# One of seven Strassen products of the up/gate stage computed by a second, inner Strassen scheme

## The chip, the cores and the metric

One NeuronCore of one Trainium2 chip runs the whole kernel. The metric is the time of one execution on the device, in microseconds (us). The kernel before took 1171.3 us, the median of three runs (1171.29 to 1173.07).

## The reference, cut to what matters

The reference is one residual block of a streaming encoder on 1024 tokens of width 1024: a normalisation, a mixer (gated DeltaNet heads and a short convolution), a second normalisation and a SwiGLU feed-forward of width 2816, then a last normalisation. The change lies in the first half of the feed-forward:

```python
def swiglu(h, w_gate, w_up, w_down):
    return (jax.nn.silu(h @ w_gate) * (h @ w_up)) @ w_down
...
h = rms_norm(x, norm2_w[l]) * (1.0 + scale2) + shift2
x = x + gate2 * swiglu(h, w_gate[l], w_up[l], w_down[l])
```

## The kernel before

**Numbers.** A float32 operand of a large matmul is split into a high part (a cast to the rounded matmul type, on ScalarE, called ACT) and a low part (the rest, a subtraction on VectorE, called DVE). A product is then three matmuls: high by high, high by low, low by high. Each has a weight load of its own.

**The up/gate stage.** The 2816 columns of w_gate and w_up are 22 tiles of 128, handled as 11 pairs p = 0 to 10. For a pair, the weights are cut into two column tiles by two inner halves (A11 to A22, 4 inner blocks k of 128 each), and the normalised tokens into two inner halves by two token halves of 512 (B11 to B22). A Strassen scheme makes the four blocks of the result with seven products instead of eight. `STEPS` (L44) lists them: step 0 is A11 x B11 into bank X, step 1 is A12 x B21 into bank Y, step 2 S2 x T2 onto X, step 3 S1 x T1 into Z, step 4 S3 x T3 onto X, step 5 S4 x B22 onto Z, step 6 A22 x T4 onto X. S1 to S4 are sums of weight blocks, T1 to T4 of token blocks. Each step is done for gate (q = 0) and up (q = 1), each into a PSUM bank of its own: `run` (L1719) issues 2 q x 4 k x 3 = 24 matmuls with 512 columns.

B11 and B21 lie in `H[0..3][0]` and `H[4..7][0]`: they are made by `first_half` (L1551), in the stage before, by transposing the normalised tokens on TensorE (PE), adding the shift and splitting (`tr_split`, L1527). The T blocks come from `sums_x` (L1541) and from `t_split` (L1700), which runs during pair 0 only, between the products of pair 0, into PSUM banks that are named by hand.

**Order of work.** From the second normalisation on there is no planner: each engine works in the order in which the program is written. Around the change that order is: the output products of the mixer (`w_out_tile`), tile by tile, with `first_half`, `early_load`, `sums_x` and the normalisation of the tiles between them; then pair 0, written out step by step with `t_split` (from L1908 on); then the loop over p = 1 to 10 (L1956), in which each step calls `run(p, s)` and then `block(p, s)` (L1790). `block` holds what DVE and ACT do while that step's products run: sums, casts (`cast`, L1672) and lows (`low`, L1678) of the weights for a later step, and the reading of the banks. `keep` (L1739) copies a bank to SBUF (ACT), `close` (L1744) adds a bank to the copy (DVE). In block 1, `keep(p, "p1", "X")` copies X after step 0; in block 2, `close(p, "p1", "Y")` adds Y after step 1, and then SiLU of the gate (ACT) and the product with up (DVE) follow. The casts and lows of A12 for pair p + 1 stand in block 6 of pair p. In block 0 of the next pair the last two banks X are read, the first by ACT, the second by DVE. Stores to DRAM and weight loads go by the SyncE queue (SP); `early_load` (L1576) uses ACT's queue. `slot` (L1689) hands out split weight tiles in a ring of eight.

Of the kernel before, what the change touches and what calls it, by code (L numbers as in the profile page):

```python
# [17 lines left out]
P = 128  # L18
# [5 lines left out]
HT = 512  # L24
# [27 lines left out]
def kernel(  # L52
# [21 lines left out]
    nc = tc.nc  # L74
    chain, mover = [None], [None]

    class Ordered:
# [18 lines left out]
    PE, DVE, ACT, POOL, SP = (Ordered(n, e) for n, e in (  # L96
        ("pe", nc.tensor), ("dve", nc.vector), ("act", nc.scalar), ("pool", nc.gpsimd), ("sp", nc.sync)))
# [7 lines left out]
    def nm(s):  # L105
        n_id[0] += 1
        return f"{s}_{n_id[0]}"
# [5 lines left out]
    cst = ctx.enter_context(tc.tile_pool(name="cst", bufs=1))  # L113
    hp_ = ctx.enter_context(tc.tile_pool(name="hp", bufs=1))
# [16 lines left out]
    def flat(ap):  # L131
        return ap.rearrange("p a b -> p (a b)")
# [37 lines left out]
    def raw_t(shape=(P, HT), dtype=F32):  # L170
        return cyclic("raw", RAW, shape, dtype)
# [372 lines left out]
    s2c = cst.tile([P, KB], F32, name="s2c", tag="s2c")  # L544
    b2c = cst.tile([P, KB], F32, name="b2c", tag="b2c")
    db2 = cst.tile([P, 4], F32, name="db2", tag="db2")
    su = []

    sim = Sim(seq, dict(pe=T_START[0], dve=T_START[1], act=T_START[2], pool=T_START[3], sp=T_START[4]))
# [794 lines left out]
    Y = [{}, {}]  # L1344
# [206 lines left out]
    def first_half(ks):  # L1551
        for k in ks:
            H[k][0] = tr_split(lambda: h_slot(k, 0), [x2n[i][:, k * P:(k + 1) * P] for i in range(4)], allb.get("tr"), b2c[:, k:k + 1])

    def w_out_tile(t, ch):
        ps = allb.get("o")
        sl = slice((t - 4) * P, (t - 3) * P)
        us = (us0, us1)[ch]
        for n, k in enumerate(KORD):
            for m, (yi, ui) in enumerate(((0, 0), (0, 1), (1, 0))):  # L1560
                pmm(ps, Y[1][k][yi][:, sl], us[k][ui], n == 0 and m == 0, n == KB - 1 and m == 2)
        cs = slice(ch * HT, (ch + 1) * HT)
        DVE.tensor_tensor(x2[t][:, cs], x2[t][:, cs], ps, ALU.add)
# [32 lines left out]
    first_half(range(4))  # L1596
    w_out_tile(5, 1)
    keep_x2(5, (1,))
    first_half(range(4, 8))
    early_load(0)  # L1600
    early_load(1)
    sums_x(0)
# [25 lines left out]
    class Weights:  # L1628
# [53 lines left out]
        def mat(self, n):  # L1682
            for q in range(2):
                self.cast(n, q)
                self.low(n, q)

    n_slot = [0]

    def slot():  # L1689
        n_slot[0] += 1  # L1690
        n = n_slot[0] - 14
        if n <= 0 or n % 8 in (5, 6, 7, 0):
            return hl_t([P, 2, 4, P])
        return mp.tile([P, 2, 4, P], F32R, name=nm("u"), tag="gl", bufs=4)
# [24 lines left out]
    def run(p, s, q_=(0, 1)):  # L1719
        b, an, bn, first = STEPS[s]  # L1720
        if first and 0 in q_:
            for q in (0, 1):
                bk[p][q][b] = bank_tile(bk[p][q][b], "acc")
        for q in q_:
            u, ps = W[p].u[an][q], bk[p][q][b]
            for k in range(4):
                x_ = B[bn][k]
                for n, (wi, xi) in enumerate(((0, 0), (0, 1), (1, 0))):
                    pmm(ps, u[:, wi, k, :], x_[:, xi, :], first and k == 0 and n == 0, k == 3 and n == 2, not first)

    def cc(p, n):
        if p == 0 and n == "p1":
# [6 lines left out]
    def keep(p, n, b):  # L1739
        cc(p, n)  # L1740
        for q in (0, 1):
            ACT.copy(c[p][n][q], bk[p][q][b])

    def close(p, n, b):  # L1744
        for q in (0, 1):
            DVE.tensor_tensor(c[p][n][q], c[p][n][q], bk[p][q][b], ALU.add)

    def silu(p, n):
        ACT.activation(c[p][n][0], c[p][n][0], AF.Silu)
# [10 lines left out]
    def store(p, n, t):  # L1760
        pend.append((am_scr[p, A_IX[n]], t))
# [28 lines left out]
    def block(p, s):  # L1790
        w, n = W.get(p), W.get(p + 1)
        last = p == NP - 1
        if s == 0:
            if p > 0:
                o = p - 1
                ACT.activation(c[o]["z5"][1], bk[o][0]["X"], AF.Silu)
            if w:
                w.sum_n("S1")
                w.sum_n("S2")
                for q in (0, 1):  # L1800
                    w.cast("S2", q)
            if p > 0:
                a12 = c[o]["z5"][1]
                DVE.tensor_tensor(a12, bk[o][1]["X"], a12, ALU.mult)
                store(o, "A12", a12)
            if w:
                for q in (0, 1):
                    w.low("S2", q)
        elif s == 1:
            if w:  # L1810
                keep(p, "p1", "X")
                w.cast("S1", 0)
                w.cast("S1", 1)
            if p > 0:
                o = p - 1
                a11, s1, a21 = c[o]["p1"][0], c[o]["p1"][1], c[o]["u2"][0]
                DVE.tensor_tensor(a11, s1, a11, ALU.subtract)
                DVE.tensor_tensor(a21, c[o]["z5"][1], a11, ALU.subtract)
                store(o, "S2", a11)
                store(o, "S4", a21)  # L1820
            if w:
                w.low("S1", 0)
                w.low("S1", 1)
                w.sum_n("S3")
        elif s == 2:
            close(p, "p1", "Y")
            w.cast("S3", 0)
            silu(p, "p1")
            w.cast("S3", 1)
            w.low("S3", 0)  # L1830
            w.low("S3", 1)
            act(p, "p1")
            store(p, "A11", c[p]["p1"][0])
            w.sum_n("S4")
        elif s == 3:
            keep(p, "u2", "X")
            w.mat("S4")
            prep_gate(p - 1)
        elif s == 4:
            keep(p, "z5", "Z")  # L1840
            w.mat("A22")
            prep_sums(p - 1)
            if last:
                first_mats(0, "A11", am_scr)
        elif s == 5:
            close(p, "z5", "X")
            if n:
                n.cast("A11", 0)
            silu(p, "z5")
            if n:  # L1850
                n.cast("A11", 1)
                n.low("A11", 0)
                n.low("A11", 1)
            act(p, "z5")
            store(p, "A22", c[p]["z5"][0])
            if last:
                first_mats(1, "B11", None)
        elif s == 6:
            close(p, "u2", "Z")
            if n:  # L1860
                n.cast("A12", 0)
            silu(p, "u2")
            if n:
                n.cast("A12", 1)
                n.low("A12", 0)
                n.low("A12", 1)
            act(p, "u2")
            a11, a21, a22, s1, s3 = c[p]["p1"][0], c[p]["u2"][0], c[p]["z5"][0], c[p]["p1"][1], c[p]["u2"][1]
            DVE.tensor_tensor(s1, a21, a22, ALU.add)
            DVE.tensor_tensor(s3, a11, a21, ALU.subtract)  # L1870
            store(p, "S1", s1)
            store(p, "S3", s3)
            if last:
                first_mats(2, "A12", am_scr)

# [48 lines left out]
    W[0].low("S2", 1)  # L1924
    t_split("T1", (6, 7, 4, 5))
    close(0, "p1", "Y")
    silu(0, "p1")
    run(0, 2, (0,))
    act(0, "p1")
# [26 lines left out]
    for p in range(1, NP):  # L1956
        for s in range(7):
            if s == 0:
                prep_load(p - 1)
            if s == 3 and p < NP - 1:  # L1960
                W[p + 1] = Weights(p + 1)
                W[p + 1].load(0)
            if s == 5 and p < NP - 1:
                W[p + 1].load(1)
            if p == NP - 1 and s in (3, 5, 6):
                first_load(*{3: (0, "A11"), 5: (1, "B11"), 6: (2, "A12")}[s])
            if s != 6:
                flush()
            run(p, s)
            block(p, s)  # L1970
    m_ctx.__exit__(None, None, None)
    dp = ctx.enter_context(tc.tile_pool(name="dp", bufs=1, side="left", reuse_waits="tile"))
# [211 lines left out]
```

## Time and profile before

| | |
|---|---|
| median of three runs | 1171.3 us |
| the profiled execution's own time | 1170.96 us |
| its span in the profile | 1169.1 us |
| instructions | 16455 |
| granted TensorE clock, mean | 0.999 |
| DVE, additions of PSUM banks (close) | 43.9 us in 66 |
| ACT, copies of banks (keep) | 38.4 us in 66 |

The profile is one execution. PE is TensorE's matmuls, PEld its weight loads, which overlap them; SP is the queue that issues DMAs. A row of the timeline gives the start in us from the span's start, the length, the engine, the line, the operation with output and inputs, and, in brackets, how long the engine had been idle and what ended the wait. Rows of one kind in a row are merged (x24); the ends of matmuls are modelled, so spacing is best read from starts. A row by groups gives busy us, mean ns of one, and idle time before.

### The profile page before, as it was taken

The numbers are of one execution on the slowest core, as the hardware profiler recorded it, in microseconds if no ns is written. First come the engines' busy times: TensorE is split into PE (matmuls) and PEld (weight loads), VectorE is DVE, ScalarE is ACT, GpSimd is POOL, SyncE is SP. The second block draws the span as 40 slices with busy tenths as digits, with TensorE's granted clock in tenths as the row PEclk, the third lists the DMA queues.
The fourth block names the chain that finished last, engine by engine and source line by source line (L and its number), as shares of the span: only waits on it lengthen the run. The fifth ranks groups of instructions, "written<-read, shape, count | busy, mean of one in ns | idle before, by whom it ended". The sixth has DMA issues, their size and how long they took to land.

```text
span 1169.1 us, 16455 instructions
## 1 busy us (share of the span) xinstructions
PE 1159.0 (99%) x5586; PEld 969.4 (83%) x5586; DVE 922.0 (79%) x1718; ACT 539.5 (46%) x1168; POOL 61.2 (5%) x100
## 2 busy tenths in 40 slices
PE   9999999999999999999999999999999999999997
PEld 7888888888888988888888888888888888888886
DVE  7998988899977998668776777776777687788676
ACT  5688733469633643325433333333333365443343
POOL 2110101002000002100000000000000000000002
PEclk9999999999999999999999999999999999999999
DMA  9624365535215554434264456446554589869413
GB/s 360 257 64 146 106 186 158 174 116 161 81 57 163 164 187 153 194 97 139 95 214 151 149 199 225 151 139 221 192 182 135 197 303 391 310 203 339 146 36 144
DMA packets 126452, 207.06 MB, mean 177 GB/s; under 512 B 20512, under 2 KB 45088, under 8 KB 126368
## 3 DMA queue, kind: packets, MB, share of 16 engines
q1 hardware_dynamic: 120992, 202.80, 51.3%
q10 hardware_dynamic: 5376, 3.21, 0.9%
q8 instruction: 44, 0.72, 0.3%
q14 instruction: 40, 0.33, 0.1%
HBM read 150.91 MB, written 55.05 MB: 176 GB/s over the span
## 4 chain that ended last, share of the span: by engine, by line
PE 92%; DVE 4%; DMA 2%; ACT 1%; issue 1%; SPq 0%; POOL 0%; DVEq 0%; ACTq 0%; POOLq 0%
PE acc L88 34%; PE acc L450 24%; PE dn L88 17%; PE o L450 4%; PE o L88 4%; PE A L450 1%; PE K L450 1%; DVE xo L89 1%; PE ab L450 1%; PE tr L450 1%; PE w L450 1%; PE u L450 1%; PE qk L450 1%; PE kk L450 1%; DMA R<-in_w_gate_dram 1%
## 5 line engine op out<-in xcount | busy, mean ns | idle before, releaser
L450 PE MATMUL acc<-h,u 128*128 128x512 f32 x1200 | 300.2, 398 | 0.0
L450 PEld LDWEIGHTS acc<-h,u 128*128 128x128 f32 x1200 | 219.2, 188 | 41.6
L88 PE MATMUL acc<-h,hl 128*128 128x512 f32 x600 | 140.1, 390 | 0.0
L88 PEld LDWEIGHTS acc<-h,hl 128*128 128x128 f32 x600 | 112.4, 188 | 23.2
L88 PE MATMUL acc<-h,u 128*128 128x512 f32 x456 | 106.1, 389 | 0.0
L88 PE MATMUL acc<-T,hl 128*128 128x512 f32 x432 | 101.4, 390 | 0.1
L88 PEld LDWEIGHTS acc<-h,u 128*128 128x128 f32 x456 | 85.6, 188 | 17.8
L88 PEld LDWEIGHTS acc<-T,hl 128*128 128x128 f32 x432 | 80.9, 188 | 17.2 <-ACT cc L89 0.5
L88 PE MATMUL dn<-h,h 128*128 128x512 f32 x396 | 90.7, 389 | 0.0
L89 DVE TENSOR_TENSOR xo<-xo,dn 128x512 f32<-128x512 f32 x84 | 57.2, 686 | 42.0 <-PE dn L88 34.6
L89 ACT COPY cc<-acc 128x512 f32<-128x512 f32 x66 | 38.4, 590 | 108.3 <-PE acc L88 108.3
L88 PEld LDWEIGHTS dn<-h,h 128*128 128x128 f32 x396 | 74.3, 188 | 15.4
L88 PE MATMUL acc<-T,u 128*128 128x512 f32 x360 | 84.0, 389 | 0.0
L88 PEld LDWEIGHTS acc<-T,u 128*128 128x128 f32 x360 | 67.6, 188 | 14.0
L89 DVE TENSOR_TENSOR cc<-cc,acc 128x512 f32<-128x512 f32 x66 | 43.9, 684 | 29.8 <-PE acc L88 29.8
L450 DVE TENSOR_TENSOR u<-raw,u 128x512 fp32r<-128x512 f32 x82 | 56.3, 688 | 12.2 <-ACT u L450 12.0
L89 DVE TENSOR_TENSOR hl<-R,hl 128x512 fp32r<-128x512 f32 x60 | 39.5, 689 | 33.5 <-ACT hl L89 33.4
L450 ACT CAST u<-raw 128x512 fp32r<-128x512 f32 x61 | 37.8, 621 | 57.8 <-PE acc L450 52.9
L450 DVE SCALAR_TENSOR_TENSOR cv<-pr,cols_a,cv 128x512 f32<-128x512 f32 x72 | 53.2, 747 | 0.3 <-ACT cv L450 0.2
L89 ACT CAST h<-rw 128x512 fp32r<-128x512 f32 x57 | 32.7, 618 | 40.9 <-PE dn L88 34.6
L89 DVE TENSOR_TENSOR u<-R,u 128x512 fp32r<-128x512 f32 x46 | 30.1, 688 | 20.5 <-ACT u L89 20.5
L89 ACT CAST hl<-R 128x512 fp32r<-128x512 f32 x60 | 35.5, 622 | 23.1 <-DVE R L89 10.7
(339 smaller groups left out, 2002.0 us busy)
## 6 DMA issues: line engine op xcount, KB each, us to landing
raw<-in_w_in_dram SPq DMA_DIRECT2D x82, 256.0 KB, 3.1
am_scr<-cc SPq DMA_DIRECT2D x77, 256.0 KB, 4.5
raw<-in_w_ada_dram SPq DMA_DIRECT2D x56, 256.0 KB, 3.2
rw<-am_scr SPq DMA_DIRECT2D x55, 256.0 KB, 5.1
rw<-bm_scr SPq DMA_DIRECT2D x53, 256.0 KB, 5.3
bm_scr<-raw SPq DMA_DIRECT2D x51, 256.0 KB, 5.4
R<-in_w_gate_dram SPq DMA_DIRECT2D x22, 512.0 KB, 3.9
R<-in_w_up_dram SPq DMA_DIRECT2D x22, 512.0 KB, 5.3
```

Source lines behind the costliest of these rows:

```text
L88: return call(*a, **k)
L89: ins = call(*a, **k)
L450: ins = call(*a, **k)
```

## The change

For p = 1 to 10, step 1 (A12 x B21 for gate and up) is done by seven smaller products m1 to m7 with 256 columns. The inner scheme cuts three ways: its rows are gate and up, its inner halves are k = 0, 1 and k = 2, 3, its columns the two token halves of 256. Pair 0 keeps its step 1. The 24 matmuls of 512 columns become 7 x 2 x 3 = 42 of 256; m1, m2, m5, m6 and m3 are issued in step 1, m7 after the q = 0 half of step 2, and m4 after its q = 1 half. They use the two banks of Y: one holds y and z (256 columns each), the other x. Four times a part is copied out by ACT between products that go onto it (K).

New operands: `inner_half` replaces `first_half(range(4, 8))` and makes, besides H[4..7][0], three sums q1, q2, q3 of token blocks of 256 with their splits; `inner_last`, in pair 0 after `close(0, "p1", "Y")`, makes q4 in the place of the second token half of H[4] and H[5]. For each pair `inner_sums` makes four sums of weight blocks (DVE) in block 6, and four casts and lows of them replace the two of A12 (three of 512 columns, one of 256). `close_inner` replaces `close` in block 2; as m4 is issued at the end of step 2, its last addition needs the end of step 2. `keep(p, "p1", "X")` moves ahead of the products of step 1. The SBUF area reserved for dynamic DMAs is made smaller.

```diff
@@ the stage before
+    HN = HT // 2
+    tq = {n: hp_.tile([P, 2, 2, HN], F32R, name=n, tag=n) for n in ("q1", "q2", "q3")}
+
+    def inner_half(a):
+        DVE.tensor_tensor(db3[:, a:a + 1], b2c[:, 6 + a:7 + a], b2c[:, 4 + a:5 + a], ALU.subtract)
+        bank = {}
+        for k in (4 + a, 6 + a):
+            bank[k] = allb.get("tr")
+            H[k][0] = tr_split(lambda: h_slot(k, 0), [x2n[i][:, k * P:(k + 1) * P] for i in range(4)], bank[k], b2c[:, k:k + 1])
+        pa, pb = bank[4 + a], bank[6 + a]
+        f12, f3 = raw_t(), raw_t()
+        f1, f2, f3 = f12[:, 0:HN], f12[:, HN:HT], f3[:, 0:HN]
+        DVE.tensor_copy(f3, pa[:, HN:HT])
+        DVE.tensor_tensor(f1, f3, pa[:, 0:HN], ALU.subtract)
+        DVE.tensor_tensor(f2, pb[:, HN:HT], f1, ALU.subtract)
+        DVE.tensor_tensor(f3, pb[:, HN:HT], f3, ALU.subtract)
+        for n, f, col in (("q1", f1, None), ("q2", f2, b2c[:, 6 + a:7 + a]), ("q3", f3, db3[:, a:a + 1])):
+            hi, lo = tq[n][:, 0, a, :], tq[n][:, 1, a, :]
+            if col is None:
+                split(f, hi, lo, DVE)
+            else:
+                ACT.activation(hi, f, AF.Identity, bias=col, scale=1.0)
+                DVE.scalar_tensor_tensor(lo, f, col, hi.bitcast(F32), ALU.add, ALU.subtract)
+
+    def inner_last():
+        for a in (0, 1):
+            t = raw_t([P, 2, HN])
+            DVE.tensor_tensor(t, H[6 + a][0][:, :, 0:HN].bitcast(F32), tq["q2"][:, :, a, :].bitcast(F32), ALU.subtract)
+            DVE.tensor_tensor(t[:, 0], t[:, 0], t[:, 1], ALU.add)
+            q4 = H[4 + a][0][:, :, HN:HT]
+            split(t[:, 0], q4[:, 0], q4[:, 1], DVE)
...
-    first_half(range(4, 8))
+    inner_half(0)
+    inner_half(1)
@@ class Weights
+        def inner_sums(self):
+            g, u = self.m["A12"]
+            L = self.L = mp.tile([P, 4, 2, P], F32, name=nm("L"), tag="L", bufs=1)
+            DVE.tensor_tensor(L[:, 0], u[:, 0:2], u[:, 2:4], ALU.add)
+            DVE.tensor_tensor(L[:, 1], L[:, 0], g[:, 0:2], ALU.subtract)
+            DVE.tensor_tensor(L[:, 3], g[:, 0:2], u[:, 0:2], ALU.subtract)
+            DVE.tensor_tensor(L[:, 2], g[:, 2:4], L[:, 1], ALU.subtract)
+            Lf = L.rearrange("p s k c -> p (s k) c")
+            self.iu = [None] * 4
+            self.src = [g, Lf[:, 0:4], Lf[:, 4:8], u[:, 2:4]]
...
@@ slot
-        n = n_slot[0] - 14
+        n = n_slot[0] - 12
@@ after run
+    INNER = {"m1": (0, 0, "x"), "m2": (0, 2, "y"), "m5": (1, 0, "z"), "m6": (1, 2, "x"), "m3": (2, 0, "z"), "m7": (2, 2, "x"), "m4": (3, 2, "x")}
...
+    def inner(p, ms):
+        if p not in iw:
+            yz, x_ = bank_tile(bk[p][0]["Y"], "acc"), bank_tile(bk[p][1]["Y"], "acc")
+            iw[p] = dict(yz=yz, y=yz[:, 0:HN], z=yz[:, HN:HT], x=x_[:, 0:HN])
+        for m in ms:
+            i, k0, d = INNER[m]
+            first = m in ("m1", "m2", "m5")
+            u = W[p].iu[i]
+            for k in range(2):
+                for n, (wi, xi) in enumerate(((0, 0), (0, 1), (1, 0))):
+                    pmm(iw[p][d], u[:, wi, k0 + k, :], inner_b(m, k, xi), first and k == 0 and n == 0, k == 1 and n == 2, not first)
+            if m in ("m1", "m5", "m6", "m7"):
+                if p not in ik:
+                    ik[p] = mp.tile([P, 4, HN], F32, name=nm("L"), tag="L", bufs=1)
+                ACT.copy(ik[p][:, {"m1": 0, "m6": 1, "m5": 2, "m7": 3}[m]], iw[p][d])
+
+    def close_inner(p, n):
+        (g, u), K, w = c[p][n], ik[p], iw[p]
+        DVE.tensor_tensor(g, g, flat(K[:, 0:2]), ALU.add)
+        DVE.tensor_tensor(u[:, HN:HT], u[:, HN:HT], K[:, 2], ALU.add)
+        DVE.tensor_tensor(g, g, w["yz"], ALU.add)
+        DVE.tensor_tensor(u[:, HN:HT], u[:, HN:HT], K[:, 3], ALU.add)
+        DVE.tensor_tensor(u[:, 0:HN], u[:, 0:HN], w["x"], ALU.add)
@@ block
-                keep(p, "p1", "X")
+                if not p:
+                    keep(p, "p1", "X")
...
-            close(p, "p1", "Y")
+            close_inner(p, "p1")
...
@@ block 6 (n is the next pair)
-                n.cast("A12", 0)
+                n.inner_sums()
+                n.inner_cast(0)
             silu(p, "u2")
             if n:
-                n.cast("A12", 1)
-                n.low("A12", 0)
-                n.low("A12", 1)
+                n.inner_cast(1)
+                n.inner_low(0)
+                n.inner_low(1)
             act(p, "u2")
...
             store(p, "S3", s3)
+            if n:
+                for i in (2, 3):
+                    n.inner_cast(i)
+                    n.inner_low(i)
@@ pair 0
     close(0, "p1", "Y")
+    inner_last()
     silu(0, "p1")
@@ the loop over pairs
-            run(p, s)
+            if s == 1:
+                keep(p, "p1", "X")
+                inner(p, ("m1", "m2", "m5", "m6", "m3"))
+            elif s == 2:
+                run(p, s, (0,))
+                inner(p, ("m7",))
+                run(p, s, (1,))
+                inner(p, ("m4",))
+            else:
+                run(p, s)
             block(p, s)
@@ kernel
-    nc = _bacc.Bacc("TRN2", target_bir_lowering=False, num_devices=1)
+    nc = _bacc.Bacc("TRN2", target_bir_lowering=False, num_devices=1, dynamic_dma_scratch_size=1024)
```

More of the change, by code (lines that the diff above doesn't have):

```diff
@@ L546 @@
     db2 = cst.tile([P, 4], F32, name="db2", tag="db2")
+    db3 = cst.tile([P, 2], F32, name="db3", tag="db3")
     su = []
@@ L1685, in mat, with inner_cast, inner_low @@
                 self.low(n, q)
+        def inner_sums(self):
[8 more added lines that the diff above has]
+            self.src = [g, Lf[:, 0:4], Lf[:, 4:8], u[:, 2:4]]
+        def inner_cast(self, i):
+            u = self.iu[i] = slot()
+            ACT.copy(u[:, 0] if i < 3 else u[:, 0, 2:4], self.src[i])
+        def inner_low(self, i):
+            u = self.iu[i]
+            hi, lo = (u[:, 0], u[:, 1]) if i < 3 else (u[:, 0, 2:4], u[:, 1, 2:4])
+            DVE.tensor_tensor(lo, self.src[i], hi.bitcast(F32), ALU.subtract)
     n_slot = [0]
@@ L1729, in run, with inner_b @@
                     pmm(ps, u[:, wi, k, :], x_[:, xi, :], first and k == 0 and n == 0, k == 3 and n == 2, not first)
+    iw, ik = {}, {}
+    INNER = {"m1": (0, 0, "x"), "m2": (0, 2, "y"), "m5": (1, 0, "z"), "m6": (1, 2, "x"), "m3": (2, 0, "z"), "m7": (2, 2, "x"), "m4": (3, 2, "x")}
+    def inner_b(m, k, xi):
+        if m in ("m1", "m4"):
+            return H[4 + k][0][:, xi, 0:HN] if m == "m1" else H[4 + k][0][:, xi, HN:HT]
+        if m in ("m2", "m3"):
+            return H[6 + k][0][:, xi, 0:HN] if m == "m2" else H[6 + k][0][:, xi, HN:HT]
+        return tq[{"m5": "q1", "m6": "q2", "m7": "q3"}[m]][:, xi, k, :]
+    def inner(p, ms):
[20 more added lines that the diff above has]
+        DVE.tensor_tensor(u[:, 0:HN], u[:, 0:HN], w["x"], ALU.add)
     def cc(p, n):
```

## The prediction

> **What bounds the kernel now.** I read the page of the profile first: its busy shares and its chain of waits.
>
> ```profile
> PE 1159.0 (99%) x5586; PEld 969.4 (83%) x5586; DVE 922.0 (79%) x1718; ACT 539.5 (46%) x1168; POOL 61.2 (5%) x100
> ...
> PE 92%; DVE 4%; DMA 2%; ACT 1%; issue 1%; SPq 0%; POOL 0%; DVEq 0%; ACTq 0%; POOLq 0%
> ```
>
> TensorE is busy for 99% of the span and carries 92% of the chain: only fewer or shorter matmuls, or a new gap on PE, can move the time. Next the timeline of the up/gate stage, from step 3 of one pair to step 3 of the next (columns: start, length in us, engine, line, operation).
>
> ```profile
> 702.47 5.60 PE L88 MATMUL acc<-h,hl 128*128 128x512 f32 x24
> ...
> 707.91 5.60 PE L88 MATMUL acc<-T,hl 128*128 128x512 f32 x24
> 708.11 0.59 ACT L89 COPY cc<-acc 128x512 f32<-128x512 f32 x1 [2.13 <-PE acc L88]
> ...
> 740.55 5.60 PE L88 MATMUL acc<-h,u 128*128 128x512 f32 x24
> ```
>
> A step of 24 matmuls takes 707.91 - 702.47 = 5.44 us, one every 226.7 ns, and a pair 740.55 - 702.47 = 38.08 = 7 x 5.44: there is no gap on PE in a pair. What a pair gains on PE is gained whole, if the other engines keep up.
>
> **The matmuls of step 1.** In ten pairs (p = 1 to 10) 24 matmuls with 512 columns go, and 7 products x 2 k x 3 = 42 with 256 columns come, each with a weight load of its own as before: 21/24 of the columns, 18 more instructions. All depends on the spacing c of a 256-column matmul, which no row shows. The nearest rows, from three stretches of the PE timeline and the groups by line:
>
> ```profile
> 11.07 1.50 PE L450 MATMUL heat<-ident,ones 128*128 128x128 f32 x12
> ```
> ```profile
> 532.67 1.91 PE L88 MATMUL tr<-ident,raw 128*128 128x128 f32 x16
> ```
> ```profile
> 481.98 2.94 PE L88 MATMUL o<-h,WQ 128*128 128x512 f32 x12
> ```
> ```profile
> 7.58 1.88 PE L88 MATMUL ps<-raw,ones 128*128 128x512 f32 x4
> ```
> ```profile
> L450 PE MATMUL heat<-ident,ones 128*128 128x128 f32 x40 | 5.0, 275 | 0.0
> ...
> L88 PE MATMUL o<-h,WQ 128*128 128x512 f32 x48 | 11.9, 396 | 0.0
> ...
> L88 PE MATMUL tr<-ident,x 128*128 128x128 f32 x88 | 11.2, 272 | 0.0
> ...
> L88 PE MATMUL ps<-raw,ones 128*128 128x512 f32 x4 | 1.9, 593 | 0.0
> ```
> ```profile
> L88 PEld LDWEIGHTS acc<-h,hl 128*128 128x128 f32 x600 | 112.4, 188 | 23.2
> ```
>
> A merged row's length is all spacings and one last duration (the means above). The heat records, each with its own weight load, start every (1.50 - 0.275)/11 = 111 ns; transposes every (1.91 - 0.272)/15 = 109 ns. So a weight load, though its record lasts 188 ns, can follow another after 109 to 111 ns: the floor of c. At 512 columns the spacing is 226.7 ns here and (2.94 - 0.396)/11 = 231 in the o products: a part of it, f, is a price per matmul and not per column, and c = (226.7 + f)/2. The heat-up's type shows a small one: 512 columns take (1.88 - 0.593)/3 = 429 ns, 128 take 111, so 0.83 ns a column and f = 5. The o products, equal in columns and type to the stage, pay some 4 ns more than the stage. Nothing bounds f better than 0 to about 25; I take the middle, 13, and c = 120. Ends for the range: 109 (transposes) and 126 (f = 25).
>
> Saved per pair: 24 x 0.2267 - 42 x 0.120 = 5.44 - 5.04 = 0.40 us; **ten pairs: -4.0 us** (-8.6 at 109, -1.5 at 126).
>
> The Trainium skill, TensorE: Matmul & The Clock Gate, section Back-to-back issue gap, gives 262 cycles for 256 columns at the warm clock, 109 ns, and 518 for 512, 216 ns. The second is not what this trace has (226.7), so I make its first a rival only; by it the saving would be 8.5 us.
>
> **Waits inside step 1 and 2.** m6 adds onto x after m1 was copied out, with 12 matmuls between; m7 and m4 have as many or more. Only m3 is close: it writes z, which holds m5, whose ACT copy must be through, and only m6 lies between: 6 x 120 = 0.72 us. ACT starts a copy 0.20 us after the product ends (707.91 to 708.11 above). For a copy of 256 columns:
>
> ```profile
> L450 ACT COPY qs<-xbd 32x256 f32<-32x256 f32 x5 | 2.0, 404 | 3.2 <-DMA xbd<-dx 3.1
> ```
> ```profile
> L450 DVE TENSOR_TENSOR L<-L,ct 128x256 f32<-128x256 f32 x8 | 3.4, 422 | 2.3 <-DMA dl<-L 2.3
> ```
>
> 0.20 + 0.40 + an assumed 0.07 to hand back = 0.67, but the weight load of m3 goes one matmul (0.12) earlier and may carry the wait: 0.07 late per pair, **+0.7 us** in ten (0 to 1.5). Queued behind it on PE are all the later products.
>
> **DVE and ACT in a pair.** New on DVE: four sums of 256 columns, 1.5 lows of 512, three 256-column additions in the close: 7 x 0.42 + 1.0 = 4.0 us; on ACT 1.5 casts and four copies, 2.5 us. One pair of before (columns: length, then busy us and instructions of PE, PEld, DVE, ACT, POOL):
>
> ```profile
> 702.50:740.60 38.10, 38.10 (x170) 31.55 (x169) 27.33 (x40) 13.40 (x24) 0.00 (x0) 1.00 0.53 180
> ```
>
> DVE would go from 27.3 of 38.1 us to 31.3 of 37.7, still under. The critical place is the DVE queue between step 6 and step 1:
>
> ```profile
> 718.99 0.69 DVE L89 TENSOR_TENSOR cc<-cc,acc 128x512 f32<-128x512 f32 x1 [2.03 <-PE acc L88]
> 719.59 1.29 DVE L89 TENSOR_TENSOR hl<-R,hl 128x512 fp32r<-128x512 f32 x2
> ...
> 722.73 1.22 DVE L89 TENSOR_TENSOR S<-R,R 128x1024 f32<-128x1024 f32 x1
> ...
> 724.23 11.04 PE L88 MATMUL acc<-h,hl 128*128 128x512 f32 x48
> ...
> 725.12 0.68 DVE L89 TENSOR_TENSOR cc<-acc,cc 128x512 f32<-128x512 f32 x1
> ...
> 727.88 0.69 DVE L89 TENSOR_TENSOR cc<-cc,cc 128x512 f32<-128x512 f32 x1
> ```
>
> m1 is first into bank X of the last pair's q = 1, which the product at 725.12 reads (before, that bank was first needed half a step later). With 1.7 us of sums and 1.0 of lows ahead of it, it ends at 725.80 + 2.7 = 728.5; step 1 starts at 724.23 + 5.44 = 729.67. **1.2 us of cover: 0.** close_inner waits for m4, the end of step 2, where close waited for step 1; the S3 lows behind it then come about 5 us later, some 1.9 us into step 3, and step 4 needs them 3.5 us later still: 0. The gate loads wait for those lows, land 4 to 5 us later and are cast two steps on: 0. The cover of all these is one step, 5.4 us.
>
> **The front: inner_half.** Its DVE operations stand between the lows of the transposes and sums_x(0). Per a: copy, three sums, three lows of 256, about 2.9 us; 5.9 in all. What DVE has free from there to the sums of pair 0's weights:
>
> ```profile
> 502.36 0.69 DVE L89 TENSOR_TENSOR x<-x,o 128x512 f32<-128x512 f32 x1 [0.24 <-PE o L88]
> ...
> 505.67 1.28 DVE L89 SCALAR_TENSOR_TENSOR x<-x,st,u 128x1024 f32<-128x1024 f32 x1 [2.63 <-POOL st L89]
> ...
> 507.94 0.69 DVE L89 TENSOR_TENSOR x<-x,o 128x512 f32<-128x512 f32 x1 [0.99 <-PE o L88]
> ...
> 513.53 0.69 DVE L89 TENSOR_TENSOR x<-x,o 128x512 f32<-128x512 f32 x1 [2.36 <-PE o L88]
> ```
> ```profile
> 519.11 0.69 DVE L89 TENSOR_TENSOR x<-x,o 128x512 f32<-128x512 f32 x1 [1.00 <-PE o L88]
> ...
> 531.33 0.69 DVE L89 TENSOR_TENSOR S<-R,R 128x512 f32<-128x512 f32 x1 [0.18 <-DMA R<-in_w_gate_dram]
> ```
>
> The waits for PE and the DMA take up the delay, 0.24 + 0.99 + 2.36 + 1.00 + 0.18 = 4.8 us; the wait of 2.63 us for the norm (POOL) does not, since it starts anew after each addition. So 5.9 - 4.8 = 1.1 us remain at 531 us (0 to 1.8).
>
> **The front: inner_last.** From there on DVE is the engine on the path. DVE and PE of pair 0:
>
> ```profile
> 542.38 1.28 DVE L89 TENSOR_TENSOR cc<-cc,acc 128x512 f32<-128x512 f32 x2
> 543.76 0.69 DVE L89 TENSOR_TENSOR cc<-cc,cc 128x512 f32<-128x512 f32 x1
> 544.37 2.72 DVE L89 SCALAR_TENSOR_TENSOR T<-tr,db,T 128x512 fp32r<-128x512 f32 x4
> 547.00 1.29 DVE L89 TENSOR_TENSOR hl<-S,hl 128x512 fp32r<-128x512 f32 x2
> 548.20 2.48 DVE L89 TENSOR_TENSOR T<-tr,T 128x512 fp32r<-128x512 f32 x4
> 550.60 1.29 DVE L89 TENSOR_TENSOR R<-R 128x512 f32<-128x512 f32 x2
> ```
> ```profile
> 546.16 1.91 PE L88 MATMUL tr<-ident,x 128*128 128x128 f32 x16
> ...
> 555.44 5.75 PE L88 MATMUL acc<-T,hl 128*128 128x512 f32 x24
> ```
> ```profile
> PEld acc L88 <- ACT cc L89: 0.5, 1, 0.5
> ```
>
> DVE has no gap from 544 to 552, and PE already waits 0.5 us at 555.44 for ACT's copies, which stand behind casts of what DVE makes at 550.60. So each microsecond added on DVE here is one on PE. inner_last goes in after the close (543.66). Per a: a sum of 512 (0.69), one of 256 (0.42), the ACT cast (0.40, DVE waits), the low (0.42), hand-overs 0.1: 2.0; twice, 4.0, and silu stands behind the second cast, 0.1. The T3 lows move from 544.37 to 544.37 + 1.1 + 4.1 = 549.6, and the T4 transposes, due at 546.16 into the banks that they free, to about 550.3. All of it reaches 555.44. **+5.2 us** (3.5 to 6.5; before 531 some of it may be hidden).
>
> The Trainium skill, the same page, section HAM oscillation — how this bites in real kernels, warns of idle gaps over about 3.4 us, after which the clock halves; the longest new gap, before the T4 transposes, is 3.2 us as estimated here, so I add nothing; before's granted clock cannot show it.
>
> **Sum.** -4.0 + 0.7 + 5.2 = +1.9 us on the profiled execution's 1170.96: 1172.9. The median of the runs is 0.3 higher: **1173.2 us**.
>
> **Rivals.** (a) *The short matmul is cheap*: c = 109 to 113.4. For it: heat-up and transposes. Against: another type. Saving 8.5 to 6.8 us, front 5.2 and hardly a wait (0.3): 1168 to 1170. (b), on the other side: *the short matmul keeps a longer hand-over*, c = 126, as where the o products are spaced at 231 after the transposes; a change of shape on PE comes four times in each pair now. Saving 1.5: +0.7 + 5.2 - 1.5 = +4.4, 1175.7. It decides above c = 122: there the sum passes +2.3 us. For it: those stretches; against: 226.7 throughout the pairs. A stall of 0.2 us per pair, as at m1 or m3, gives as much. (c) *A weight load isn't hidden under so short a matmul*: c = 188, 42 x 0.188 = 7.90, +2.5 per pair, +24.6 + 5.2: 1201. Against: the heat-up has 111. (d) *Pair 0 hides its DVE work*, front about 1: 1168.5. Against: the 0.5 us wait at 555.44. (e) *The step isn't shortened*, because the work is not done as said: the products are written out one by one, so hardly.
>
> **Chances.** Forecast (1171.5 to 1175) 0.40; (a) 0.20; (b) 0.27; (c) 0.05; (d) 0.06; (e) 0.02. About 0.2%, 2.3 us, can be told from no change. Slower, above 1173.6: 0.16 of the forecast, all of (b) and (c): 0.48. Faster, below 1169.0: 0.08 of (a), 0.03 of (d): 0.11. Same: 0.41. Range 1168 to 1179: outside are (c) and the edges of (a), (b), (d), some 0.15. The forecast's own range is 1171.5 to 1175.
>
> **What would show it.** A pair from step 3 to step 3 of about 37.7 us, the short matmuls 120 ns apart; 5 us of PE gaps between 541 and 561 us, most before the T4 transposes; nothing before m1, under 0.1 us before m3. Wrong it would be by another c, by PE reaching step 4 of pair 0 on time, or by a gap in every pair.

## The result, and the profile after

The changed kernel takes 1176.43 us, the median of seven runs (1173.21 to 1177.27), against 1171.69 us in seven runs of the kernel before on the same chip: a ratio of 1.0035, with a 95% interval of 1.0025 to 1.0045. It is slower: by the ratio about 4.1 us (2.9 to 5.3); the two medians alone are 4.7 us apart. The profiled execution took 1174.57 us, its span is 1172.8 us, and its mean granted clock is 0.997 (before: 1170.96 us, 1169.1 us, 0.999). So the profiled pair differs by 3.6 us, and this is the difference that the trace is asked about. The profiled execution of the changed kernel is 1.9 us faster than its median; what the slower executions add is in no trace here.

The page of the profile after, the busy row and the chain of waits:

```profile
PE 1158.0 (99%) x5766; PEld 975.0 (83%) x5766; DVE 961.7 (82%) x1830; ACT 564.3 (48%) x1236; POOL 61.7 (5%) x100
...
PE 51%; DVE 3%; ACT 1%; issue 1%; DMA 0%; POOL 0%; DVEq 0%; ACTq 0%; POOLq 0%
```

There are 180 more matmuls (10 pairs x 18), yet PE is busy 1.0 us less, while the span is 3.7 us longer. So PE now stands still 4.7 us more than before, in places that are still to be found. The busy share, 99% in both kernels, shows none of it, and the chain covers only about half of the span here, so neither answers the question. The timeline does.

**In a pair the change does what it should.** PE of the changed kernel, from step 1 of one pair to step 1 of the next (in this and the later views, the row at the end of a stretch that was asked for can be cut short, as x11 or x8 instead of x24):

```profile
697.73 1.59 PE L88 MATMUL acc<-h,u 128*128 128x256 f32 x12
...
701.32 2.90 PE L88 MATMUL acc<-T,hl 128*128 128x512 f32 x12
704.05 0.88 PE L88 MATMUL acc<-q,u 128*128 128x256 f32 x6
704.77 2.91 PE L88 MATMUL acc<-T,hl 128*128 128x512 f32 x12
707.51 0.88 PE L88 MATMUL acc<-h,u 128*128 128x256 f32 x6
708.23 5.63 PE L88 MATMUL acc<-h,hl 128*128 128x512 f32 x24
713.70 5.60 PE L88 MATMUL acc<-T,u 128*128 128x512 f32 x24
...
735.46 1.60 PE L88 MATMUL acc<-h,u 128*128 128x256 f32 x12
```

A pair takes 735.46 - 697.73 = 37.73 us, where it took 38.08: 0.35 us less. The 30 short matmuls of step 1 take 701.32 - 697.73 = 3.59 us, one every 119.7 ns, and m7 and m4 0.72 us each. The stretches of 512 columns next to them take 2.73, 2.74 and 5.47 us instead of 2.72, 2.72 and 5.44: some 0.06 us a pair goes at the changes of shape. So 5.44 - 3.59 - 0.72 - 0.72 - 0.06 = 0.35, and ten pairs save 3.5 us.

**In the front the time is lost.** DVE of the changed kernel, from the sums of pair 0's weights to the lows of T3, then the sums of R:

```profile
533.14 0.68 DVE L89 TENSOR_TENSOR S<-R,R 128x512 f32<-128x512 f32 x1
...
545.36 0.68 DVE L89 TENSOR_TENSOR raw<-h,q 128x512 f32<-128x512 f32 x1
...
546.97 0.42 DVE L89 TENSOR_TENSOR h<-raw,h 128x256 fp32r<-128x256 f32 x1 [0.47 <-ACT h L89]
...
550.07 2.72 DVE L89 SCALAR_TENSOR_TENSOR T<-tr,db,T 128x512 fp32r<-128x512 f32 x4
...
556.30 1.28 DVE L89 TENSOR_TENSOR R<-R 128x512 f32<-128x512 f32 x2
```

and PE, around the T4 transposes and at step 4 of pair 0:

```profile
544.71 3.01 PE L88 MATMUL acc<-T,hl 128*128 128x512 f32 x12
...
550.87 3.58 PE L88 MATMUL tr<-ident,x 128*128 128x128 f32 x16 [3.15 <-DVE T L89]
...
558.74 3.02 PE L88 MATMUL acc<-h,hl 128*128 128x512 f32 x12
561.59 2.66 PE L88 MATMUL acc<-T,hl 128*128 128x512 f32 x11
```

The sums come at 533.14 instead of 531.33, 1.8 us late: that is inner_half and a wait behind it. The lows of T3 come at 550.07 instead of 544.37, 5.7 us late: inner_last added 3.9 us. PE stands still for 3.15 us for them, and step 4 starts at 561.59 instead of 555.44, 6.15 us late.

The last 0.45 of the 6.15 us are PE's own. Windows of the changed kernel (columns: length, then busy us of PE, PEld, DVE, ACT and POOL, granted clock, DMA share, GB/s):

```profile
548.00:551.00 3.00, 0.13 (x1) 0.13 (x2) 2.39 (x6) 2.51 (x5) 0.00 (x0) 1.00 0.00 0
551.00:554.00 3.00, 3.00 (x15) 2.96 (x16) 3.00 (x6) 3.00 (x7) 0.00 (x0) 0.50 0.25 93
554.00:558.00 4.00, 4.00 (x24) 3.47 (x23) 4.00 (x7) 1.75 (x4) 0.00 (x0) 0.95 0.67 206
```

After the still time the clock is halved for some 3.4 us (all of the second window, and 5% lost of the third: 0.4 us at half), and the 16 transposes take 3.58 us instead of 1.91. The last matmul ahead of the still time started at 544.71 + 3.01 - 0.39 = 547.33, the first transpose at 550.87: 3.54 us apart, with 3.15 us of idle time between them by the profile, where the ends of matmuls are modelled. The rule of the Trainium skill that the prediction weighed (TensorE: Matmul & The Clock Gate, HAM oscillation — how this bites in real kernels) warns of idle gaps over about 3.4 us. This trace agrees with it if the gap is counted from start to start; by the profile's idle time the clock halved after less. Most of the half clock's price is hidden, since DVE is late on its own account: from the sums of R to step 4 it is 555.44 - 550.60 = 4.84 us before and 561.59 - 556.30 = 5.29 us after. And PE, not DVE, now decides: 558.74 + 12 x 0.2267 = 561.46 is the end of its product.

**Pair 1 pays a wait that no other pair has.** DVE and PE at its step 1:

```profile
581.31 1.22 DVE L89 TENSOR_TENSOR S<-R,R 128x1024 f32<-128x1024 f32 x1
582.56 1.23 DVE L89 TENSOR_TENSOR S<-S,R 128x1024 f32<-128x1024 f32 x1
583.71 0.68 DVE L89 TENSOR_TENSOR cc<-acc,cc 128x512 f32<-128x512 f32 x1
...
584.44 1.70 PE L88 MATMUL acc<-h,u 128*128 128x256 f32 x12 [0.93 <-DVE cc L89]
```

m1 may not write the bank before DVE's product with the last bank X of pair 0 has read it, at 584.39. The waits of PE list this once, with 0.9 us; between the starts of the matmuls it is 1.1 us more than the spacing.

The sum: 6.15 + 1.1 - 3.5 = 3.75 us, against 3.7 us in the spans. Nothing is left over in the profiled pair.

### The profile page after: what moved, and what is told of

Its sections match the earlier page's. It is cut to its first block, busy times and chain, and to the rows that moved or that the text cites. A ratio compares the mean times of both kernels' runs of the same rounds, so it can differ in the third digit from the quotient of the medians.

```text
span 1172.8 us, 17025 instructions
## 1 busy us (share of the span) xinstructions
PE 1158.0 (99%) x5766; PEld 975.0 (83%) x5766; DVE 961.7 (82%) x1830; ACT 564.3 (48%) x1236; POOL 61.7 (5%) x100
## 4 chain that ended last, share of the span: by engine, by line
PE 51%; DVE 3%; ACT 1%; issue 1%; DMA 0%; POOL 0%; DVEq 0%; ACTq 0%; POOLq 0%
PE acc L88 33%; PE dn L88 17%; DVE xo L89 1%; DVE cc L89 1%; PE tr L88 0%; DVE h L89 0%; DVE x L89 0%; DVE S L89 0%; DMA x_scr<-x 0%; DVE hl L89 0%; DVE raw L89 0%; DVE T L89 0%; DVE u L89 0%; ACT jf L89 0%; ACT hl L89 0%
## 5 line engine op out<-in xcount | busy, mean ns | idle before, releaser
L450 PE MATMUL acc<-h,u 128*128 128x512 f32 x1200 | 300.4, 398 | 0.0
L88 PE MATMUL acc<-T,hl 128*128 128x512 f32 x552 | 131.3, 390 | 0.0
L88 PEld LDWEIGHTS acc<-T,hl 128*128 128x128 f32 x552 | 102.2, 188 | 20.3
L88 PE MATMUL acc<-h,u 128*128 128x256 f32 (+1 forms) x480 | 89.7, 336 | 0.9 <-DVE cc L89 0.9
L88 PE MATMUL acc<-T,u 128*128 128x512 f32 x240 | 56.0, 389 | 0.0
L88 PEld LDWEIGHTS acc<-T,u 128*128 128x128 f32 x240 | 45.0, 188 | 9.4
L89 ACT CAST hl<-S 128x512 fp32r<-128x512 f32 x44 | 25.3, 622 | 57.0 <-DVE S L89 57.0
L89 DVE TENSOR_TENSOR hl<-S,hl 128x512 fp32r<-128x512 f32 x44 | 28.5, 687 | 27.7 <-ACT hl L89 26.4
L89 ACT CAST u<-R 128x512 fp32r<-128x512 f32 (+1 forms) x60 | 34.0, 582 | 35.5 <-DVE R L89 35.2
L89 ACT ACTIVATE cc<-cc 128x512 f32<-128x512 f32 x33 | 20.9, 632 | 62.5 <-DVE cc L89 62.5
```

Of the source, the lines that this page charges most:

```text
L88: return call(*a, **k)
L89: ins = call(*a, **k)
L450: ins = call(*a, **k)
```

## The experiments

Theory A: the loss is DVE work put on the path of pair 0 (and the wait of pair 1), while the pairs themselves gain 0.35 us each. Rival B: the loss sits in the pairs, and the front is no more than a shift that comes back later. Rival C: most of the loss is the half clock. Each ratio is to the kernel before on the same chip, with its 95% interval; the median of the kernel before was 1171.59 us for e1, e2, e3 and e5 (24 runs) and 1171.78 us for the other four (21 runs).

### e1: the new operands of the front alone

Against the changed kernel: every pair runs the plain step 1; the result of inner_last goes to q1's place, where nothing reads it.

```diff
-            q4 = H[4 + a][0][:, :, HN:HT]
+            q4 = tq["q1"][:, :, a, :]
...
-            if s == 1:
-                keep(p, "p1", "X")
-                inner(p, ("m1", "m2", "m5", "m6", "m3"))
...
+            run(p, s)
...
-            close_inner(p, "p1")
+            close(p, "p1", "Y")
```

> The front's work alone: inner_half and inner_last stay (q4 goes to a place of its own, so that H[4] and H[5] stay whole), all pairs do step 1 with 24 matmuls of 512 columns as before. Theory A (the loss is DVE work on the path of pair 0, the gain is 0.35 us in each of ten pairs): about 6 us slower than the kernel before, with a PE gap of over 3 us ahead of the T4 transposes and a stretch at half clock behind it. Rival B (the loss lies in the pairs): the time of the kernel before, within 1 us.

Measured: 1177.31 us, 1.0046 (1.0033 to 1.0059), 5.4 us slower than before, and without the pairs' gain slower than the whole change as a median. DVE's lows, the T4 transposes and step 4 of pair 0 in e1:

```profile
549.66 2.72 DVE L89 SCALAR_TENSOR_TENSOR T<-tr,db,T 128x512 fp32r<-128x512 f32 x4
```
```profile
550.47 3.10 PE L88 MATMUL tr<-ident,x 128*128 128x128 f32 x16 [3.15 <-DVE T L89]
...
561.36 1.98 PE L88 MATMUL acc<-T,hl 128*128 128x512 f32 x8
```

Step 4 is 5.9 us late, and stays so: the down projection starts at 958.5 us in e1 and 952.7 before. The shift, 5.8 us there, doesn't come back, so the second half of rival B falls.

### e2: the inner scheme in the pairs alone

first_half stands where inner_half was, and inner_last is left out: q1 to q3 are zeros from POOL and q4 isn't made, so the seven products are issued on other numbers and the output is not the reference's.

```diff
-    inner_half(0)
-    inner_half(1)
+    first_half(range(4, 8))
...
-    inner_last()
...
+    for t in tq.values():
+        POOL.memset(t.bitcast(F32), 0.0)
```

> The pairs' part alone: step 1 of pairs 1 to 10 by the seven products, but the token sums q1 to q3 are zeros written by GpSimd, and q4 is left out (H[4] and H[5] stay as they are), so the work of inner_half and inner_last is missing. Theory A: 3.5 us of saving less about 1 us of a wait before m1 of pair 1: 2 to 3.5 us faster than before. Rival B: as slow as the changed kernel, 4 to 5 us slower than before.

Measured: 1169.08 us, 0.9977 (0.9968 to 0.9986), 2.7 us faster than before. PE at step 4 of pair 0 and at step 1 of pair 1:

```profile
555.95 5.73 PE L88 MATMUL acc<-T,hl 128*128 128x512 f32 x24 [0.15 <-ACT cc L89]
...
578.93 1.70 PE L88 MATMUL acc<-h,u 128*128 128x256 f32 x12 [0.93 <-DVE cc L89]
```

The front is back to within 0.5 us, the wait of pair 1 is there, and 3.5 - 1.1 = 2.4 us is what is left. The other numbers change nothing in the pairs: from m1 of pair 1 to the down projection it is 371.94 us here (578.93 to 950.87), and 371.94 us in the changed kernel (584.44 to 956.38). Rival B falls: the pairs gain.

### e3: inner_last in pair 1

The scratch tile of `inner_last` moves to another buffer.

```diff
-            t = raw_t([P, 2, HN])
+            t = wst.tile([P, 2, HN], F32, name=nm("qt"), tag="aacc", bufs=1)
...
-    inner_last()
     silu(0, "p1")
...
                 store(o, "S4", a21)
+                if p == 1:
+                    inner_last()
```

> inner_last is moved out of pair 0 to step 1 of pair 1, where DVE has a wait to fill; all else as changed. Theory A: the 3.9 us of DVE work leave the path, the gap before the T4 transposes falls under 2 us, no half clock: about 5 us faster than the changed kernel, within 1 us of the kernel before. Rival B: as the changed kernel, since the same work is done.

Measured: 1171.06 us, 0.9993 (0.9984 to 1.0002): no difference that can be told. DVE's lows of T3, and step 4 of pair 0 in e3:

```profile
546.00 2.72 DVE L89 SCALAR_TENSOR_TENSOR T<-tr,db,T 128x512 fp32r<-128x512 f32 x4
```
```profile
557.05 5.74 PE L88 MATMUL acc<-T,hl 128*128 128x512 f32 x24 [0.49 <-ACT cc L89]
```

Both are 1.6 us late, which is what inner_half and the wait behind it leave. q4 is first read by m4, at the end of step 2 of pair 1, and made there in time it costs nothing. The sum, 1.6 + 1.1 - 3.5 = -0.8 us, is what the ratio gives, though its interval reaches past no change.

### e5: filler ahead of the T4 transposes

The changed kernel with 12 float32 matmuls (24 rows in the trace) where PE stands still, into a bank of the T4 transposes ahead of them; nothing reads what they leave there. If rival C holds, most of the loss goes.

```diff
+    fill_ = bank_tile(2, "fill")
+    for _ in range(12):
+        pe("pe", PE.matmul(fill_[:, 0:P], ones, ident, start=True, stop=True))
     t_split("T4", (6, 7, 2, 3))
```

> The changed kernel with 12 plain fp32 matmuls of 128 columns (24 records, some 2.7 us, on constants, results unused) put into PE's gap ahead of the T4 transposes. If the clock halves because of PE's idle time, the clock stays full, and the gap of useful work stays. Theory A (DVE sets the end of pair 0, the half clock adds little): 0.3 to 1.5 us faster than the changed kernel, and the spread of its runs narrower. Rival C (the half clock is most of the loss): 3 us faster or more. If the spread stays as wide, it is not from the clock.

Measured: 1174.31 us, 1.0024 (1.0014 to 1.0033). The norm of e5 that stands behind inner_half, and DVE's sums of R:

```profile
519.04 1.28 DVE L89 SCALAR_TENSOR_TENSOR x<-x,st,u 128x1024 f32<-128x1024 f32 x1 [2.80 <-DMA x_scr<-x]
...
555.32 1.28 DVE L89 TENSOR_TENSOR R<-R 128x512 f32<-128x512 f32 x2
```
```profile
546.58 2.84 PE L88 MATMUL fill<-ident,ones 128*128 128x128 f32 x24
...
549.89 2.19 PE L88 MATMUL tr<-ident,x 128*128 128x128 f32 x16 [0.46 <-DVE T L89]
...
560.14 3.24 PE L88 MATMUL acc<-T,hl 128*128 128x512 f32 x13 [0.60 <-ACT cc L89]
```

The filler keeps the clock up: the transposes take 2.19 us, not 3.58. Step 4 comes 1.45 us earlier than in the changed kernel, but 1.0 of that was already there at the sums of R (555.32 instead of 556.30), where the clock has no part; it comes from a shorter wait of a norm (2.80 us instead of 3.91). From the sums of R to step 4 it is 4.82 us, as before, instead of 5.29: the half clock costs 0.47 us, and rival C falls as "most". The times of the two kernels can't tell so little. Their spread did not get clearly narrower, as had been expected if it came from the clock: 3.4 us here, 4.1 in the changed kernel.

### e4: q from H, in pairs 0 to 2, and the inner scheme from pair 2

first_half is back, q1 to q3 are made on DVE from the split H during pairs 0 and 1, q4 in pair 2, and pairs 0 and 1 run the plain step 1.

```diff
-    inner_half(0)
-    inner_half(1)
+    first_half(range(4, 8))
...
+    def inner_late(a):
...
+        DVE.tensor_tensor(xa, ha[:, 0].bitcast(F32), ha[:, 1].bitcast(F32), ALU.add)
+        DVE.tensor_tensor(f2, hb[:, 0].bitcast(F32), hb[:, 1].bitcast(F32), ALU.add)
+        DVE.tensor_tensor(f1, f3, f1, ALU.subtract)
+        DVE.tensor_tensor(f3, f2, f3, ALU.subtract)
+        DVE.tensor_tensor(f2, f2, f1, ALU.subtract)
+        for n, f in (("q1", f1), ("q2", f2), ("q3", f3)):
+            split(f, tq[n][:, 0, a, :], tq[n][:, 1, a, :], DVE)
...
             W[0].mat("A22")
+            inner_late(0)
...
+            if p == 1 and s == 2:
+                inner_late(1)
```

> Pairs 0 and 1 run the plain step 1, pairs 2 to 10 the inner scheme; q1 to q3 are made on DVE from the split H during pairs 0 and 1, and q4 in pair 2, so inner_half and inner_last are gone from the front. Theory A (the whole loss is DVE work put ahead of pair 0, the pairs gain 0.35 us each): step 4 of pair 0 starts as in the kernel before, within 0.5 us; the half clock ahead of it goes; nine pairs give 9 x 0.35 = 3.1 us; no wait of 1 us in pair 1: 1168.5 beside 1171.6, ratio 0.9973, and below the variant with the pairs alone, which keeps that wait. Theory B (the inner pairs gain nothing as a whole, and the variant with the pairs alone was faster for what it left out): 1171 to 1172. Theory D (DVE is too full in pairs 0 and 1, so that the moved work only moves the wait): a new gap on PE of 1 us or more in pair 0, 1 or 2, 1170 or more.

Measured: 1169.10 us, 0.9978 (0.9968 to 0.9987): 2.6 us faster than the kernel before, and the fastest of the kernels here that leave nothing out. DVE at the first sums after the transposes of the front, and PE in pair 0:

```profile
500.38 0.68 DVE L89 TENSOR_TENSOR x<-x,x 128x512 f32<-128x512 f32 x1
```
```profile
556.31 5.74 PE L88 MATMUL acc<-T,hl 128*128 128x512 f32 x24 [0.17 <-ACT cc L89]
...
567.61 5.69 PE L88 MATMUL acc<-T,hl 128*128 128x512 f32 x24
```

Step 4 of pair 0 is 0.9 us later than before, more than expected; 0.9 us is what the first row is late too (499.51 before), ahead of all that e4 moves. From step 4 to the down projection (950.8 us) it is 394.5 us, against 397.3 before: 2.8 us saved, of the 9 x 0.35 = 3.15 expected. The rest is in pair 0, where two matmuls around 567.6 us come 0.36 us late: theory D in a small size, as far as can be seen, though the profile names no releaser there. There is no wait of 1 us at the first m1, which is in pair 2 here.

### e6 and e7: the price of a short matmul by itself

The kernel before, with step 1 of pairs 1 to 10 cut into columns of 256 (e6) or 128 (e7).

```diff
+            cw = 256 if p and s == 1 else HT
+            for c0 in range(0, HT, cw):
...
-                    pmm(ps, u[:, wi, k, :], x_[:, xi, :], first and k == 0 and n == 0, k == 3 and n == 2, not first)
+                        pmm(ps[:, c0:c0 + cw], u[:, wi, k, :], x_[:, xi, c0:c0 + cw], first and k == 0 and n == 0, k == 3 and n == 2, not first)
```

> The kernel before, where step 1 of pairs 1 to 10 runs each of its 24 products with 512 columns as two with 256 (48 matmuls, the same sums, the same result, no inner scheme). It measures the spacing of a 256-column matmul by itself, with 24 more of them in a pair. At the 119.5 ns seen in the changed kernel a step is 48 x 0.1195 = 5.74 us instead of 5.44: +0.30 a pair, +3.0 us, about 1174.6. At the 126 ns of rival (b) +0.61 a pair, +6.1 us. If the 119.5 held hand-overs of the inner scheme and the matmul alone were 113.4 (half of 226.7): no change, 1171.6.

> The same with 128 columns: 96 matmuls in step 1 of pairs 1 to 10. If a matmul costs a fixed 12 ns and 0.418 ns a column (the line through 226.7 at 512 and 119.5 at 256), a step is 96 x 0.066 = 6.3 us, +0.9 a pair, +9 us: about 1181. If the weight load sets a floor of 109 to 111 ns, as the heat-up and the transposes show with 128 columns, a step is 96 x 0.110 = 10.6 us, +5.1 a pair, +51 us: about 1223, and then 119.5 ns at 256 columns is only some 9 ns above that floor.

Measured: e6 1175.13 us, 1.0032 (1.0020 to 1.0043), 3.7 us slower; e7 1225.99 us in one run. Step 1 of a pair in e6, then steps 0 and 1 of a pair in e7:

```profile
769.99 5.92 PE L88 MATMUL acc<-h,hl 128*128 128x256 f32 x48
775.74 5.63 PE L88 MATMUL acc<-T,hl 128*128 128x512 f32 x24
```
```profile
747.24 16.27 PE L88 MATMUL acc<-h,hl 128*128 128x512 f32 x120
763.35 5.71 PE L88 MATMUL acc<-T,u 128*128 128x512 f32 x24
```

With 256 columns it is 5.75 / 48 = 119.8 ns, the same as in the inner scheme; with 128, (16.11 - 5.44) / 96 = 111.1 ns. From 512 to 256 columns 107 ns go, from 256 to 128 only 8.7: there is a floor of about 111 ns, the spacing that the prediction read from the heat-up, and 256 columns lie just above it. That the weight load sets the floor is argued and not shown, since in every run each of these matmuls has one. In time e6 costs 3.7 us, where 24 more matmuls at this spacing give 10 x 0.31 = 3.1: within its interval.

### e8: another order of the products

e3 with the products of step 1 in another order, so that the first product into bank X of the last pair comes 12 matmuls later.

```diff
-                inner(p, ("m1", "m2", "m5", "m6", "m3"))
+                inner(p, ("m2", "m5", "m1", "m3", "m6"))
```

> The variant with inner_last in pair 1, and in step 1 the products in the order m2, m5, m1, m3, m6 instead of m1, m2, m5, m6, m3, so that the first product into bank X of the last pair comes 12 matmuls (1.4 us) later. Theory A with the second loss (m1 of pair 1 waits 1.1 us for DVE's reading of that bank): the wait goes, and nothing else moves: 1.1 us below that variant's 1171.1, 1170.0. Rival: DVE is late in pair 1 for other reasons and the wait only moves to the next product that needs DVE or ACT (m3, now 6 matmuls behind m5's copy with m1 between, or step 2): 1171.1, with a gap of about 1 us further on.

Measured: 1171.33 us, 0.9995 (0.9987 to 1.0004), the same as e3. Pair 1 of e8, DVE, ACT and PE together:

```profile
581.13 0.68 DVE L89 TENSOR_TENSOR cc<-acc,cc 128x512 f32<-128x512 f32 x1
581.25 1.14 ACT L89 CAST hl<-S 128x512 fp32r<-128x512 f32 x2 [4.99 <-DVE S L89]
...
582.21 0.88 PE L88 MATMUL acc<-h,u 128*128 128x256 f32 x6
582.29 1.06 ACT L89 COPY cc<-acc 128x512 f32<-128x512 f32 x2
...
583.25 0.65 ACT L89 COPY L<-acc 128x256 f32<-128x256 f32 x2
583.68 0.77 PEld L88 LDWEIGHTS acc<-h,u 128*128 128x128 f32 x6 [0.80 <-ACT L L89]
```

m1 (582.21) no longer waits, but m3 does: it needs m5's copy, and that stands on ACT behind the copies of this pair's two banks X (`keep`, 512 columns each, 1.06 us), which stand behind casts that waited 4.99 us for DVE's sums. 583.68 - 582.21 - 0.72 = 0.75 us of the 1.1 are still there. The rival held: DVE is late in pair 1, and the wait moved on. A pair has 37.79 us in this order (732.74 to 770.53), 0.06 more than in the other; ten of them take back the rest.

## Why the prediction was right, and where it wasn't

The forecast was 1.9 us more on the profiled time; measured were 3.6 us there and 4.1 by the ratio of the runs. The time lies in the range of the prediction, above the forecast's own range of 1171.5 to 1175, and on the side that had the largest chance. The mechanism was the one predicted, a gain per pair less DVE work on pair 0's path; what missed were sizes, two waits and the clock. That the errors partly cancel, a wait too many at m3 against others too few, is luck.

| step of the prediction | predicted, us | shown, us |
|---|---|---|
| ten pairs, short matmuls | -4.0 | -3.5 |
| m3 waits for m5's copy | +0.7 | 0 |
| m1 waits for DVE, pair 1 | 0 | +1.1 |
| inner_half, what is left of it | +1.1 | +1.8, 1.3 of it a longer wait for a store |
| inner_last | +4.1 | +3.9 |
| half clock | 0 | +0.45 |
| sum | +1.9 | +3.8 |

**The short matmul.** The spacing was taken as (226.7 + f)/2 with f in the middle of its bounds, 13 ns, above a floor of 109 to 111 ns: 120 ns. It is 119.8 (e6), which would be f = 12.9. e7 bears out the floor: by f and the columns alone 128 columns would take 66 ns, and it has 111. The heat-up's 111 could not show it by itself, since 128 of its columns take 107 ns as it is (429/4). That f lies in the middle of bounds as wide as 0 to 25 is luck; 119.8 lies so near the floor that e6 and e7 don't show whether it is a price per matmul. Rival (a) falls by the 119.8. The Trainium skill's 262 cycles for 256 columns, 109 ns (TensorE: Matmul & The Clock Gate, Back-to-back issue gap), are not met here either. What was missing is the 0.06 us a pair at the changes of shape, 0.6 us in ten: without them the pairs would have saved 4.1. (c) falls too: the weight load, whose record lasts 188 ns, is passed every 111 ns in e7.

**m3.** m5's copy in a middle pair, and PE at m3:

```profile
737.81 0.37 ACT L89 COPY L<-acc 128x256 f32<-128x256 f32 x1 [1.01 <-PE acc L88]
```
```profile
738.33 0.88 PE L88 MATMUL acc<-h,u 128*128 128x256 f32 x6
```

The copy ends at 738.18, 0.15 us ahead of m3. The working gave 0.67 us for copy and hand-over against 0.72 of cover, which was right; the 0.07 us of delay was put down to the weight load's earlier wait, which isn't seen.

**m1.** "1.2 us of cover: 0" was worked out in a middle pair, and there it holds. In pair 1 it doesn't, and the kernel before shows that already. PE at steps 0 and 1 of its pair 1, and DVE's product with the last bank X of pair 0:

```profile
571.91 11.04 PE L88 MATMUL acc<-h,hl 128*128 128x512 f32 x48
```
```profile
577.74 0.68 DVE L89 TENSOR_TENSOR cc<-acc,cc 128x512 f32<-128x512 f32 x1
```

Step 1 begins at 571.91 + 5.44 = 577.35, and the bank is read until 578.42, 1.07 us later: harmless before, since the bank was first needed half a step on, and the wait of m1 after. In the middle pair that the prediction shows the same product comes 0.9 us after the start of step 0; here, as DVE comes out of pair 0, 5.8 us. e2 shows that the wait has nothing to do with inner_half or inner_last; e4, where pair 2 is the first with the inner scheme, has none.

**inner_half.** The first addition behind it, in the changed kernel and before:

```profile
505.07 0.69 DVE L89 TENSOR_TENSOR x<-x,x 128x512 f32<-128x512 f32 x1
```
```profile
499.51 0.68 DVE L89 TENSOR_TENSOR x<-x,x 128x512 f32<-128x512 f32 x1
```

It takes 5.6 us of DVE, predicted 5.9, and the waits for PE were used up as reckoned. What failed is "the wait of 2.63 us for the norm (POOL) does not, since it starts anew after each addition": the wait was taken as constant. The norm of the changed kernel, and the same norm before:

```profile
520.02 1.28 DVE L89 SCALAR_TENSOR_TENSOR x<-x,st,u 128x1024 f32<-128x1024 f32 x1 [3.91 <-DMA x_scr<-x]
```
```profile
516.82 1.29 DVE L89 SCALAR_TENSOR_TENSOR x<-x,st,u 128x1024 f32<-128x1024 f32 x1 [2.60 <-POOL st L89]
```

The norm overwrites x in place, so it also waits until keep_x2's store of x has read it. Before, POOL's statistics came last; now the store does, 1.3 us later, and without that some 0.5 us of inner_half would be left. The wait varies with the run: 2.80 us in e5 and 4.83 in e8. The lows of T3 and step 4 move with it: e8, with the same front as e3, has this norm 1.8 us later (521.68 and 519.86), the lows as much (547.82 and 546.00) and step 4 too (558.88 and 557.05).

The traces show what goes along with it. DVE's delay moves the store, on ACT's queue, to the moment at which SP issues a 512 KB load of R (`in_w_gate`):

| kernel | store issued at | load issued at | the store lands after, us |
|---|---|---|---|
| before | 514.25 | 516.12 | 2.0 |
| e5 | 516.27 | 516.32 | 2.6 |
| changed | 516.15 | 516.09 | 3.8 |
| e3 | 515.97 | 515.88 | 3.8 |
| e1 | 515.77 | 515.65 | 3.7 |
| e8 | 516.88 | 516.58 | 4.7 |

On the whole, the later the store is issued, measured from the load, the longer it takes. That the load slows it is likely by this order, but not shown: no run moves the load.

**inner_last** came out as worked out: a sum, a half sum, a cast and a low, each with its wait for ACT, twice. It is 4.1 us on DVE (545.36 to 549.46), 0.2 of which DVE stood still there before: 3.9 more. That each microsecond on DVE is one on PE there is shown by e3, which moves it: the lows come 4.1 us earlier than in the changed kernel (546.00 for 550.07), and step 4 of pair 0 4.5 us earlier (557.05 for 561.59), the half clock's share with it.

**The clock.** The gap was put at 3.2 us of idle time and held against 3.4, so nothing was added. Its size was right, 3.15; the clock halved all the same, and in e1, with the same 3.15, too. Only from start to start, 3.54, does the gap lie above. The price, 0.45 us, is small because DVE's own lateness hides the rest.

**The rivals.** (b), 1175.7, lies nearest to the median, but not by its mechanism: there is no spacing of 126 ns, and of a stall in every pair only the 0.06 us at the changes of shape, where it needed 0.2. Its bound, c = 122, should have been 121: there 0.7 + 5.2 - 3.6 = 2.3 us. (d) falls by e1. (e) falls by the count of matmuls.

## What to carry to other kernels

A cheaper inner loop has to pay for its operands, and where they are made decides: the same sums make DVE 5.7 us late at the place where one engine sets the pace of a short start-up stage, and cost PE under 0.4 us when they are spread over the first turns of the loop, besides the one turn that then runs without them (0.35 us). Work out cover in the first turn of the loop as well as in a middle one, since the queues come out of the start-up late. A delay can also move a transfer beside another one, and a wait that was taken as constant can then grow. And before fewer columns are bought with more matmuls, look for the floor of a single matmul: here half the columns cost 53% of the time, a quarter of them 49%.

## What the runs showed of the hardware

- A matmul in the rounded type, with a weight load of its own, was spaced 226.7 ns at 512 columns, 119.8 at 256 and 111.1 at 128.
- About 3.5 us between two matmul starts (3.15 us idle by the profile) were followed, about a microsecond or less after the second, by some 3.4 us at half clock, in the changed kernel and in e1; with the filler, or with 0.5 us of still time (e3), there was none.
- A 256 KB store on ACT's queue landed after 2.0 us where it was issued 1.9 us ahead of a 512 KB load on SP's queue, after 2.6 to 3.8 us where the two were issued within 0.12 us, and after 4.7 us where it came 0.3 us behind the load. The cause was not tested.
